# Finishing a batch earlier and splitting a closing check in a log-sum-exp kernel

## The chip, the cores and the metric

The kernel runs on one core of a Trainium2 chip. The metric is device time in microseconds (us). The kernel before took 325.64 us (median of three runs, 325.55 to 325.72).

## What is computed

```python
x_heads = x.reshape(B, S, H, Dh).transpose(0, 2, 1, 3) + bias[None, :, None, :]
x_tiled = np.repeat(x_heads, 2, axis=2)
mx = x_tiled.max(axis=-1, keepdims=True)
lse = mx.squeeze(-1) + np.log(np.exp(x_tiled - mx).sum(axis=-1))
```

B = 8 batches, S = 2048 rows, H = 8 heads of Dh = 256 elements, all float32. For every row and head the logarithm of the sum of exponentials is wanted, and every result is stored twice, side by side. The input has 134 MB, the output 1 MB.

## The kernel before

**Tiles.** A tile is 256 rows: 128 partitions with K = 2 rows each, 2048 elements a row. There are T = 64 tiles, eight to a batch, so batch 6 is tiles 48 to 55 and batch 7 is tiles 56 to 63. SyncE issues all loads into a ring of eight tile buffers (`xb`), and reloads a buffer when its last users are done.

**Work on a tile.** No maximum is subtracted. For some heads TensorE adds the bias: a matmul puts the bias into a bank of PSUM (L336 or L353) and a second one adds x through an identity matrix (L394 or L371). ScalarE then takes the exponential of that bank and sums it through its accumulator (L405, L425). For the other heads of early tiles GpSimd adds the bias (L444) and VectorE sums (L469). In late tiles ScalarE takes the exponential of raw x (L450), and VectorE multiplies by exp(bias) and sums in one instruction for each head (L485, with a read of the accumulator after it). The last head or two go to GpSimd, which multiplies and folds (L501, L509), and VectorE sums the remaining 32 columns (L515). The table `STAGES` gives the shares by tile. From tile 57 on each of the two rows of a partition is a piece of its own (57k0, 57k1 and so on). ScalarE reads the PSUM banks of a piece after the exponential of the next piece. The last tile has eight transfers, with heads loaded in groups.

**Sums.** All sums of a batch collect in a tile `R`: `R0` for batches 0 to 3, `R1` for 4 and 5, `R2` for 6, `R3` for 7. `R3` is ordered by head, tile of the batch, row (k). A group is finished by TensorE transposes, a ScalarE logarithm that writes each result twice, and a store. The first two groups are finished in the stream (`finish`, L529 and L539) and stored after tile 61 (`store`, L544, on SyncE's queue). Batch 6 is finished after the last tile, in `turn_two` (L643) and `finish_two` (L654), and stored from SyncE at L655. Batch 7 is finished in `finish_last` (L663, L670) and stored from ScalarE's queue at L671.

**Closing check.** Since no maximum is subtracted, the kernel checks the range of all sums at the end, and would compute everything again by the safe formula (`all_again`) if it were too wide. `ends_of(i)` takes the maximum (L559) and the minimum (L562) of tile `R`i, as integers, together with those handed on from the tile before, which stand in one padding column at each side of `R`i. The last pair goes to `ends`. `judge` combines them (L578), brings them to one partition with a matmul (L586) and reduces (L587). Then every engine loads the verdict into a register (L590) and branches (L789), and the program ends (L816).

**Order.** The order on every engine is the order of the program text (`manual_schedule`); only semaphores hold engines against each other. `for_pe` and `for_pool` hold work that is put behind the start of the next piece. PSUM has four banks `ps[0..3]` (two tiles `pair` of two banks each), used in turn through the counter `n_ps`. `on_bank` tells the framework that users of different banks of a pair do not depend on each other. `tp` is another bank, for the transposes and for matmuls that only keep TensorE's clock up (L385).

Of the kernel before, what the change touches and what calls it, by code (L numbers as in the profile page):

```python
# [9 lines left out]
F32 = mybir.dt.float32  # L10
BF16 = mybir.dt.bfloat16
I32 = mybir.dt.int32
ACT = mybir.ActivationFunctionType
ALU = mybir.AluOpType
# [3 lines left out]
K = 2  # L18
# [46 lines left out]
def kernel(  # L65
# [6 lines left out]
    nc = tc.nc  # L72
    P = nc.NUM_PARTITIONS
    B, S, D = x.shape
    H, Dh = bias.shape
    assert D == H * Dh and S % (P * KB) == 0
    NBLK = S // (P * K)
    NB = S // (P * KB)
    TB = KB // K
    T = B * NBLK  # L80
# [8 lines left out]
    sb = ctx.enter_context(tc.tile_pool(name="sb", bufs=1))  # L89
# [17 lines left out]
    ends = sb.tile([P, 2], F32, name="ends")  # L107
# [3 lines left out]
    NR = KB * H * NB  # L111
# [3 lines left out]
        starts.append(min(starts[-1] + P // (H * NB), B - 2))  # L115
    groups = list(zip(starts, starts[1:]))
    widths = [(b1 - b0) * NR for b0, b1 in groups] + [NR, NR]
    Rx = [sb.tile([P, 1 + n + 1], F32, name=f"R{i}") for i, n in enumerate(widths)]
    sums_in = [r[:, 1 : 1 + n] for r, n in zip(Rx, widths)]
    R = [  # L120
        r.rearrange("p (k b h n) -> p k b h n", k=KB, h=H, n=NB)[:, :, i]
        for r, (b0, b1) in zip(sums_in, groups)
# [8 lines left out]
    res_two = sb.tile([H * NBLK, P, K, 2], F32, name="res_two")  # L131
    res_last = sb.tile([P, P, 2], F32, name="res_last")
# [7 lines left out]
    ps = [p[:, c : c + MM] for p in pairs for c in (0, MM)]  # L140
    tp = pp.tile([P, KB, P], F32, name="tp")

    def modes_of(t):
        return [modes for t0, modes in STAGES if t0 <= t][-1]
# [92 lines left out]
    for set_idx, (_name, funcs) in enumerate(get_activation_tables(nc.m.arch).items()):  # L237
        if ACT.Exp in funcs and ACT.Ln in funcs:
            nc.scalar.add_instruction(
                mybir.InstLoadActFuncSet(  # L240
                    name=nc.get_next_instruction_name(),
# [30 lines left out]
    for i, c in enumerate(range(G0, D, MM)):  # L272
# [6 lines left out]

    nc.vector.memset(Rx[0][:, 0:1], 1.0)  # L280
    nc.vector.memset(Rx[0][:, 1 + widths[0] :], 1.0)
    nc.vector.memset(one_bits, float(ONE_BITS))
    nc.vector.tensor_reduce(
        out=b_far,
        in_=brow,
        op=ALU.max,
        axis=mybir.AxisListType.X,
# [3 lines left out]
        out=Rx[0][0:1, 1 + widths[0] :],  # L291
# [11 lines left out]
    def other_factors():  # L303
        nc.scalar.activation(
            out=w_ps[:, W_LATE - W0 :], in_=b_rep[:, W_LATE - G0 : W2 - G0], func=ACT.Exp
        )
        nc.scalar.activation(out=w_sb, in_=b_rep[:, W1 - G0 :], func=ACT.Exp)


    n_ps = [0]  # L310
# [4 lines left out]
    def on_bank(i, ins):  # L315
        for j, u in bank_users[i // 2]:
            if j != i and u.ins.engine != ins.ins.engine:
                tc.declare_no_dep(ins.ins, u.ins, reason="another bank")
        bank_users[i // 2].append((i, ins))
        return ins  # L320
# [220 lines left out]
    def store():  # L541

        for (b0, b1), r in zip(groups, res):
            nc.sync.dma_start(  # L544
                out=out[b0:b1].rearrange("b h (n r) -> (b h n) r", n=NB),
                in_=r.rearrange("q p k r -> q (p k r)"),
            )

    def ends_of(i):


        bits = Rx[i].bitcast(I32)
        last = i == len(Rx) - 1
        if not last:
            low = Rx[i + 1][:, 0:1].bitcast(I32)
            high = Rx[i + 1][:, 1 + widths[i + 1] :].bitcast(I32)
        else:
            low, high = ends[:, 0:1], ends[:, 1:2]
        nc.vector.tensor_reduce(  # L559
            out=high, in_=bits[:, 1:], op=ALU.max, axis=mybir.AxisListType.X  # L560
        )
        nc.vector.tensor_reduce(  # L562
            out=low,
            in_=bits[:, 0 : 1 + widths[i]],
            op=ALU.min,
            axis=mybir.AxisListType.X,
            negate=last,
        )

    def begin_row():  # L570
        row = one_ps[0:1, 0:P]
# [25 lines left out]
    def all_again():  # L597
# [10 lines left out]
        with tc.For_i(0, B, 1) as b, tc.For_i(0, S // P, 1) as n:  # L608
# [29 lines left out]
                out=outs[at].rearrange("b n p h r -> (b n p) h r"), in_=both  # L638
            )

    def turn_two():
        for k in range(K):
            nc.tensor.transpose(  # L643
                out=tp[0 : H * NBLK, 1 + k],
                in_=R[B - 2][:, k].rearrange("p h n -> p (h n)"),
                identity=ident,
            )

    def finish_two():
        two = tp[0 : H * NBLK, 1]  # L650
        tv = bass.AP(
            tensor=two.tensor, offset=two.offset, ap=[two.ap[0], [1, P], [P, K], [0, 2]]
        )
        nc.scalar.activation(out=res_two, in_=tv, func=ACT.Ln)  # L654
        nc.sync.dma_start(  # L655
            out=out[B - 2].rearrange("h (n r) -> (h n) r", n=NBLK),
            in_=res_two.rearrange("q p k r -> q (p k r)"),
        )

    def finish_last():  # L660
        bank = n_ps[0] % len(ps)
        last = ps[bank][:, 0:P]
        turn = nc.tensor.transpose(  # L663
            out=last, in_=R_last.rearrange("p h n k -> p (h n k)"), identity=ident
        )
        on_bank(bank, turn)
        tv = bass.AP(
            tensor=last.tensor, offset=last.offset, ap=[last.ap[0], [1, P], [0, 2]]
        )
        on_bank(bank, nc.scalar.activation(out=res_last, in_=tv, func=ACT.Ln))  # L670
        nc.scalar.dma_start(  # L671
            out=out[B - 1].rearrange("h (n r) -> (h n) r", r=2 * P),
            in_=res_last.rearrange("q p r -> q (p r)"),
        )


    def sums_of(t):

        b, blk = divmod(t, NBLK)
        if b < B - 2:  # L680
            return R[b][:, blk % TB * K :, :, blk // TB]
        if b == B - 2:
            return R[b][:, :, :, blk]
        return R_last[:, :, blk, :].rearrange("p h k -> p k h")
# [20 lines left out]
    for t in range(T):  # L705
        if t == T_FACTORS:
            other_factors()
        xt = xts[t % NBUF]
        sums = sums_of(t)
        for k0, k1, c0, c1 in pieces(t):  # L710
            m = modes_of(t)[k0]
            add = None
            heads = []
            if c0 == 0:
                bias_here = bias_there
            if m["late"]:
                pe_part = late_heads(m, t, bias_here, sums)
            else:
                heads = add_x(m, t, k0, c0, c1, bias_here)

                def pe_part(t=t, heads=heads, sums=sums):
                    for k, h, bank, p, mm in heads:
                        sum_biased(t, k, h, bank, p, mm, sums)

            if c0 == 0:
                if next_units and not m["late"]:
                    bias_there = put_bias(*next_units.pop(0))
                if t > T_PROMPT and m["g0"] == H:
                    keep_warm()
                if m["g0"] < H:  # L730
                    add = g_add(m, t, k0, k1)
                if t < T - 1 or k0 == 0:
                    flush(for_pool)
            h0 = max(c0 // Dh, m["pe"])
            h1 = min(c1 // Dh, m["g0"])
            hf = max(h0, min(h1, H - m["fold"]))
            if h0 < h1 and not m["late"]:
                done = exp_inplace(
                    t, xt[:, k0:k1, h0 * Dh : h1 * Dh], loads[t, k0, c0]
                )  # L740
                if hf < h1:
                    for_pool.append(fold(t, k0, hf, h1, sums, done))
            if c0 == 0:
                flush(for_pe)
            if not m["late"]:
                for k in range(k0, k1):
                    for h in range(h0, hf):
                        weigh(
                            t,
                            xt[:, k, h * Dh : (h + 1) * Dh],  # L750
                            h,
                            sums[:, k, h : h + 1],
                            done,
                        )

            def pool_part(t=t, m=m, k0=k0, k1=k1, sums=sums, add=add):
                if add:
                    later(m, t, k0, k1, sums, add)
                if k1 == K:
                    reload(t)  # L760

            for_pool.append(pool_part)
            if m["g0"] < H:
                pe_part()
                if t == T_PROMPT - 1:
                    first_factors()
                if m["late"]:
                    bias_there = put_bias(*next_units.pop(0))
            elif heads:
                for_pe.append(pe_part)  # L770

        for i, (_, b1) in enumerate(groups):
            if t - 2 == b1 * NBLK - 1:
                finish(i)
                ends_of(i)
        if t == T - 3:
            ends_of(len(groups))
            store()
    row = begin_row()
    flush(for_pe)  # L780
    flush(for_pool)
    turn_two()
    finish_two()
    finish_last()
    ends_of(len(groups) + 1)
    again = judge(row) > SPAN_BITS

    order.__exit__(None, None, None)
# [32 lines left out]
```

## Time and profile before

| | |
|---|---|
| time of the runs, median (range) | 325.64 us (325.55 to 325.72) |
| time of the profiled execution | 325.63 us |
| its span, first to last instruction | 323.6 us |
| DMA, mean over the span | 418 GB/s; loads 98.2% of 16 engines' time |
| busy: VectorE, GpSimd, ScalarE, TensorE | 289.1, 287.1, 263.7, 248.0 us |
| last load of x on its way to SBUF until | 317.62 us |
| closing check's last VectorE instruction ends | 320.98 us |
| stores of batch 6 and batch 7, issue to landing | 2.5 and 2.3 us |

Times in the text are microseconds from the start of the span, in that one profiled execution. PE is TensorE, PEld its weight loads, DVE VectorE, ACT ScalarE, POOL GpSimd, SP SyncE; a q behind the name means the engine's instruction queue. L485 is line 485 of the kernel before. A row of the timeline gives start, duration, engine, line, operation, output and input; the note in brackets is idle time of the engine before it and what ended it. On one engine an instruction may start before the one in front of it has ended, so that the distance from start to start, not the duration, is what an instruction costs the next one.

### The profile page before, as it was taken

The page shows a single profiled execution, that of the slowest core. Times are in us where ns is not written, and L with a number is a line of the kernel's source. Part 1 is how long each engine was busy: PE and PEld are TensorE (multiplying, and loading weights), DVE is VectorE, ACT ScalarE, POOL GpSimd, SP SyncE. Part 2 cuts the span into 40 slices and gives each one's busy share as a digit, 9 for nine tenths or more (in the row PEclk, how much of TensorE's full clock was granted, in tenths as well). Part 3 has the DMA queues.
Part 4 walks back from the last instruction along what each step waited for, and adds up shares of the span by engine and source line. Part 5 has one row for each costly group of instructions (what it writes and reads, how often), then busy time and mean ns, then how long its engine had stood idle before and what let it go on. Part 6 is the DMA issues. An engine that isn't in the chain of part 4 may idle for free.

```text
span 323.6 us, 2260 instructions
## 1 busy us (share of the span) xinstructions
PE 248.0 (77%) x601; PEld 98.6 (30%) x601; DVE 289.1 (89%) x322; ACT 263.7 (81%) x422; POOL 287.1 (89%) x121
## 2 busy tenths in 40 slices
PE   5998885877886667887868876987787686398774
PEld 2333332323332223332323332333233322132231
DVE  2337999699989999979999999799999999999996
ACT  1159976798688878598889878799988999889995
POOL 7939997999999999999999989999999999858864
PEclk9979996899799999598999997899999999679998
DMA  7999999999999999999999999999999999999994
GB/s 309 462 397 454 446 398 452 437 405 454 437 405 454 434 407 450 433 413 447 437 406 454 433 407 454 409 423 431 433 425 424 421 438 420 415 421 420 423 401 149
DMA packets 8880, 135.44 MB, mean 418 GB/s; under 512 B 1057, under 2 KB 1441, under 8 KB 2465
## 3 DMA queue, kind: packets, MB, share of 16 engines
q1 hardware_dynamic: 8624, 135.14, 98.2%
q10 hardware_dynamic: 242, 0.14, 0.2%
q8 instruction: 5, 0.08, 0.1%
q14 instruction: 9, 0.07, 0.1%
HBM read 134.23 MB, written 1.05 MB: 418 GB/s over the span
## 4 chain that ended last, share of the span: by engine, by line
DMA 48%; POOL 17%; DVE 15%; PE 10%; ACT 9%; issue 0%; SPq 0%; DVEq 0%
DMA xb<-in_x_dram 48%; POOL xb L444 17%; DVE R L469 11%; ACT xb L450 7%; PE pair L394 4%; PE one_ps L394 2%; DVE xb L462 2%; DVE xb L485 2%; PE pair L336 1%; PE pair L268 1%; ACT xb L412 1%; PE one_ps L336 1%; ACT xb L405 1%; DMA brow<-in_bias_dram 1%; ACT res L539 0%
## 5 line engine op out<-in xcount | busy, mean ns | idle before, releaser
L444 POOL TENSOR_TENSOR xb<-xb,b_rep 128x2048 f32<-128x2048 f32 x57 | 256.8, 4532 | 21.5 <-DMA xb<-in_x_dram 21.5
L469 DVE TENSOR_REDUCE R<-xb 128x14 f32<-128x3584 f32 (+1 forms) x57 | 216.8, 3804 | 1.9
L450 ACT ACTIVATE xb<-xb 128x2560 f32<-128x2560 f32 (+5 forms) x77 | 157.4, 2055 | 20.7 <-POOL xb L444 20.1
L394 PE MATMUL pair<-xb,ident 128*128 128x512 f32 x216 | 111.3, 641 | 0.0
L394 PE MATMUL one_ps<-xb,ident 128*128 128x512 f32 x108 | 62.8, 665 | 18.7 <-DMA xb<-in_x_dram 18.7
L412 ACT ACTIVATE xb<-pair 128x1024 f32<-128x1024 f32 x54 | 55.5, 1028 | 19.1 <-PE pair L394 19.0
L394 PEld LDWEIGHTS pair<-xb,ident 128*128 128x128 f32 x216 | 44.6, 206 | 58.7 <-issue 58.7
L462 DVE TENSOR_TENSOR xb<-xb,w_ps 128x512 f32<-128x512 f32 x54 | 36.7, 680 | 23.0 <-ACT xb L450 23.0
L336 PE MATMUL one_ps<-b,ones_bf 128*128 128x512 bf16 x52 | 20.3, 390 | 36.7 <-ACT xb L405 36.6
L405 ACT ACTIVATE xb<-one_ps 128x256 f32<-128x256 f32 x108 | 39.9, 378 | 7.8 <-PE one_ps L394 7.8
L336 PEld LDWEIGHTS <-ones_bf 128*128 128x128 bf16 (+1 forms) x174 | 17.6, 102 | 86.3 <-issue 79.5
L336 PE MATMUL pair<-b,ones_bf 128*128 128x512 bf16 x104 | 31.2, 381 | 0.0
L371 PE MATMUL pair<-xb,ident 128*128 128x512 f32 (+1 forms) x36 | 21.6, 686 | 12.2 <-DMA xb<-in_x_dram 12.2
L394 PEld LDWEIGHTS one_ps<-xb,ident 128*128 128x128 f32 x108 | 19.9, 201 | 33.4 <-DMA xb<-in_x_dram 27.1
L485 DVE CUSTOM_DVE_ANT_0 xb<-xb,w_ps 128x256 f32<-128x256 f32 x61 | 22.3, 415 | 0.0
L405 ACT ACTIVATION_READ_ACCUMULATOR xb<-one_ps 128x1 f32 x108 | 22.0, 204 | 0.0
L509 POOL TENSOR_TENSOR xb<-xb 128x128 f32<-128x128 f32 (+3 forms) x39 | 13.9, 356 | 3.1
L501 POOL TENSOR_TENSOR xb<-xb,w_sb 128x256 f32<-128x256 f32 (+1 forms) x13 | 10.0, 772 | 5.4 <-ACT xb L450 5.0
L371 PEld LDWEIGHTS pair<-xb,ident 128*128 128x128 f32 x36 | 6.1, 208 | 23.8 <-DMA xb<-in_x_dram 23.3
L425 ACT ACTIVATE xb<-pair 128x256 f32<-128x256 f32 x33 | 12.5, 397 | 0.0
L385 PE MATMUL tp<-b_rep,ident 128*128 128x384 f32 x28 | 11.3, 486 | 0.0
L485 DVE CUSTOM_DVE_ANT_0 xb<-xb,one_ps 128x256 f32<-128x256 f32 x27 | 10.6, 413 | 0.1
(60 smaller groups left out, 72.0 us busy)
## 6 DMA issues: line engine op xcount, KB each, us to landing
xb<-in_x_dram SPq DMA_DIRECT2D x20, 4096.0 KB, 22.1
xb<-in_x_dram SPq DMA_DIRECT2D x17, 2048.0 KB, 22.4
xb<-in_x_dram SPq DMA_DIRECT2D x12, 1024.0 KB, 22.5
xb<-in_x_dram SPq DMA_DIRECT2D x5, 256.0 KB, 11.4
xb<-in_x_dram SPq DMA_DIRECT2D x2, 384.0 KB, 15.8
out_dram<-res SPq DMA_DIRECT2D x1, 512.0 KB, 6.5
out_dram<-res SPq DMA_DIRECT2D x1, 256.0 KB, 6.7
out_dram<-res_two SPq DMA_DIRECT2D x1, 128.0 KB, 2.5
```

Source lines behind the costliest of these rows:

```text
L336: nc.tensor.matmul(p, lhsT=lhsT, rhs=each_row(b, h * Dh, Dh, K), start=i == 0, stop=False,)
L371: mm = nc.tensor.matmul(p, lhsT=ident, rhs=xts[t % NBUF][:, ka:kb, c : c + w], start=False, stop=True,)
L394: mm = nc.tensor.matmul(p, lhsT=ident, rhs=xts[t % NBUF][:, :, h * Dh : (h + 1) * Dh], start=False, stop=True,)
L405: act = nc.scalar.activation(out=xts[t % NBUF][:, k, 0:Dh], in_=got[0][:, k * Dh : (k + 1) * Dh], func=ACT.Exp, accum_out=sums[:, k, 0:1],)
L412: act = nc.scalar.activation(out=xts[t % NBUF][:, :, Dh : m["pe"] * Dh].rearrange("p k (h j) -> p h k j", j=Dh), in_=got[-1].rearrange("p ...
L425: act = nc.scalar.activation(out=xts[t % NBUF][:, k, h * Dh : (h + 1) * Dh], in_=p, func=ACT.Exp, accum_out=sums[:, k, h : h + 1],)
L444: add = nc.gpsimd.tensor_tensor(out=v, in0=v, in1=each_row(b_rep, c - G0, D - c, k1 - k0), op=ALU.add)
L450: return on_x(t, nc.scalar.activation(out=v, in_=v, func=ACT.Exp), [after])
L462: mul = nc.vector.tensor_tensor(out=f, in0=f, in1=each_row(w_ps, m["pe"] * Dh - W0, n, k1 - k0), op=ALU.mult,)
L469: red = nc.vector.tensor_reduce(out=sums[:, k0:k1, h0:H], in_=v.rearrange("p k (h j) -> p k h j", j=Dh), op=ALU.add, axis=mybir.AxisListTy ...
L485: ttr = nc.vector.tensor_tensor_reduce(out=v, in0=v, in1=w, scale=1.0, scalar=0.0, op0=ALU.mult, op1=ALU.add, accum_out=dst,)
L509: done = nc.gpsimd.tensor_tensor(out=v[:, :, 0:n], in0=v[:, :, 0:n], in1=v[:, :, n : 2 * n], op=ALU.add)
```

## The change

- Batch 6 is transposed at the end of the loop's step for tile 59 and its logarithm taken at the end of the step for tile 60. The transposes write to a bank of the ring of four, not to `tp`, so that every later use of the ring moves on by one bank. The store joins the two others in `store`, after tile 61.
- `R3` gets 16 padding columns on each side in place of one, and is set to 1.0 at the start. Its maximum and minimum are taken in two halves: after tile 61 over the columns of tiles 56 to 59, directly behind the pair that hands over batch 6, and at the end over tiles 60 to 63. Each half reads a view of nine groups of eight columns, of which one group is padding with the value handed on.

```diff
-    Rx = [sb.tile([P, 1 + n + 1], F32, name=f"R{i}") for i, n in enumerate(widths)]
+    pads = [1] * (len(widths) - 1) + [NBLK * K]
+    Rx = [sb.tile([P, pad + n + pad], F32, name=f"R{i}") ...
+    nc.vector.memset(Rx[-1], 1.0)
...
+        nc.sync.dma_start(
+            out=out[B - 2].rearrange("h (n r) -> (h n) r", n=NBLK),
+            in_=res_two.rearrange("q p k r -> q (p k r)"),
+        )
...
+    def ends_of_last(half):
+        bits = Rx[-1].bitcast(I32)
+        n = NBLK * K
+        c = half * n // 2
+        views = [
+            bass.AP(
+                tensor=bits.tensor,
+                offset=bits.offset + c0 + c,
+                ap=[bits.ap[0], [n, H + 1], [1, n // 2]],
+            )
+            for c0 in (0, n)
+        ]
+        if half == 0:
+            c = n // 2
+            to = [bits[:, c0 + c : c0 + c + 1] for c0 in (0, n + NR)]
         else:
+            to = [ends[:, 0:1], ends[:, 1:2]]
+        min_max(*views, *to, mybir.AxisListType.XY, last=half == 1)
...
     def turn_two():
+        bank = n_ps[0] % len(ps)
+        n_ps[0] += 1
+        two_in.append(bank)
         for k in range(K):
-            nc.tensor.transpose(
-                out=tp[0 : H * NBLK, 1 + k],
+            turn = nc.tensor.transpose(
+                out=ps[bank][0 : H * NBLK, k * P : (k + 1) * P],
                 in_=R[B - 2][:, k].rearrange("p h n -> p (h n)"),
                 identity=ident,
             )
+            on_bank(bank, turn)
...
+        if t == T - 5:
+            turn_two()
+        if t == T - 4:
+            finish_two()
         if t == T - 3:
             ends_of(len(groups))
+            ends_of_last(0)
             store()
     row = begin_row()
     flush(for_pe)
     flush(for_pool)
-    turn_two()
-    finish_two()
     finish_last()
-    ends_of(len(groups) + 1)
+    ends_of_last(1)
```

`min_max` is a maximum and a minimum by VectorE, one instruction each, as in `ends_of` before. `finish_last` loses its two `on_bank` notes.

More of the change, by code (lines that the diff above doesn't have):

```diff
@@ L117 @@
     widths = [(b1 - b0) * NR for b0, b1 in groups] + [NR, NR]
-    Rx = [sb.tile([P, 1 + n + 1], F32, name=f"R{i}") for i, n in enumerate(widths)]
-    sums_in = [r[:, 1 : 1 + n] for r, n in zip(Rx, widths)]
+    pads = [1] * (len(widths) - 1) + [NBLK * K]
+    Rx = [
+        sb.tile([P, pad + n + pad], F32, name=f"R{i}")
+        for i, (n, pad) in enumerate(zip(widths, pads))
+    ]
+    sums_in = [r[:, pad : pad + n] for r, n, pad in zip(Rx, widths, pads)]
     R = [
@@ L547, in store, with min_max @@
             )
+        nc.sync.dma_start(
+            out=out[B - 2].rearrange("h (n r) -> (h n) r", n=NBLK),
+            in_=res_two.rearrange("q p k r -> q (p k r)"),
+        )
+    def min_max(low_in, high_in, low, high, axis, last=False):
+        nc.vector.tensor_reduce(out=high, in_=high_in, op=ALU.max, axis=axis)
+        nc.vector.tensor_reduce(out=low, in_=low_in, op=ALU.min, axis=axis, negate=last)
     def ends_of(i):
         bits = Rx[i].bitcast(I32)
[L553 to L556, printed above, removed]
-        else:
[L558 to L568, printed above, removed]
+        at = pads[i + 1] + widths[i + 1]
+        min_max(
+            bits[:, 0 : 1 + widths[i]],
+            bits[:, 1:],
+            Rx[i + 1][:, 0:1].bitcast(I32),
+            Rx[i + 1][:, at : at + 1].bitcast(I32),
+            mybir.AxisListType.X,
+        )
[8 more added lines that the diff above has]
+                ap=[bits.ap[0], [n, H + 1], [1, n // 2]],
+            )
+            for c0 in (0, n)
+        ]
+        if half == 0:
+            c = n // 2
+            to = [bits[:, c0 + c : c0 + c + 1] for c0 in (0, n + NR)]
+        else:
+            to = [ends[:, 0:1], ends[:, 1:2]]
+        min_max(*views, *to, mybir.AxisListType.XY, last=half == 1)
     def begin_row():
@@ L639, in all_again @@
             )
+    two_in = []
     def turn_two():
+        bank = n_ps[0] % len(ps)
+        n_ps[0] += 1
+        two_in.append(bank)
         for k in range(K):
-            nc.tensor.transpose(
-                out=tp[0 : H * NBLK, 1 + k],
+            turn = nc.tensor.transpose(
+                out=ps[bank][0 : H * NBLK, k * P : (k + 1) * P],
                 in_=R[B - 2][:, k].rearrange("p h n -> p (h n)"),
@@ L647, in turn_two @@
             )
+            on_bank(bank, turn)
     def finish_two():
-        two = tp[0 : H * NBLK, 1]
+        (bank,) = two_in
+        two = ps[bank][0 : H * NBLK]
         tv = bass.AP(
@@ L653, in finish_two @@
         )
[L654 to L658, printed above, removed]
+        on_bank(bank, nc.scalar.activation(out=res_two, in_=tv, func=ACT.Ln))
     def finish_last():
@@ L662, in finish_last @@
         last = ps[bank][:, 0:P]
-        turn = nc.tensor.transpose(
+        nc.tensor.transpose(
             out=last, in_=R_last.rearrange("p h n k -> p (h n k)"), identity=ident
         )
-        on_bank(bank, turn)
         tv = bass.AP(
@@ L669, in finish_last @@
         )
-        on_bank(bank, nc.scalar.activation(out=res_last, in_=tv, func=ACT.Ln))
+        nc.scalar.activation(out=res_last, in_=tv, func=ACT.Ln)
         nc.scalar.dma_start(
```

## The prediction

> **What bounds the kernel now.** I read the page's time slices first. The DMA row is full up to the last slice, so for 317 us the stream of loads sets the pace; the change does not touch the loads. It touches the last 20 us, so I read the chain that ended last there, then the timelines of ScalarE and VectorE around the places where work goes in, and last what follows the closing check.
>
> ```profile
> DMA  7999999999999999999999999999999999999994
> ```
>
> The chain of waits, in order of time (start, duration, what):
>
> ```profile
> 292.50 19.89 DMA xb<-in_x_dram
> 312.38 0.02 issue
> 312.41 1.71 ACT xb L450
> 314.11 0.02 issue
> 314.14 0.42 DVE xb L485
> ...
> 319.71 0.29 DVE ends L559
> 320.00 0.20 DVE ends L562
> 320.21 0.02 issue
> 320.23 0.17 DVE far L578
> 320.40 0.04 issue
> 320.45 0.23 PE one_ps L586
> 320.68 0.02 issue
> 320.70 0.28 DVE verdict L587
> ```
>
> Piece 62k1 lands at 312.38, its exponential ends at 314.11, and from 314.14 VectorE works without a break through 62k1 and tile 63 until the check. So the end is: landing, one exponential, 5.5 us of VectorE, check. A delay of VectorE at 314.14 goes to the end in full; a delay before 314.14 only beyond the slack there.
>
> The timeline of VectorE shows that slack:
>
> ```profile
> 311.54 0.28 DVE L562 TENSOR_REDUCE R<-R 128x1 int32<-128x129 int32 x1
> 311.74 0.17 DVE L515 TENSOR_REDUCE R<-xb 128x1 f32<-128x32 f32 x1
> 311.83 0.41 DVE L485 CUSTOM_DVE_ANT_0 xb<-xb,one_ps 128x256 f32<-128x256 f32 x1
> ...
> 313.87 0.18 DVE L515 TENSOR_REDUCE R<-xb 128x1 f32<-128x32 f32 x1
> 314.14 0.42 DVE L485 CUSTOM_DVE_ANT_0 xb<-xb,one_ps 128x256 f32<-128x256 f32 x1
> ```
>
> L515 costs the next instruction 0.09 (311.74 to 311.83). After the L515 at 313.87 VectorE could go on at 313.96; it goes on at 314.14, held by ScalarE. **Slack 0.18 us.**
>
> Behind the check (ending 320.98) come the register loads (DVE's, the longest, 957 ns from 321.02), the branches, and SyncE's closing waits (L816). In the trace these stand 0.06 apart from 322.59 to 322.65, but the eighth, on ScalarE's store of batch 7, stands at 322.77, after 0.13: that store lands at 322.76. So the store holds the end by 0.07, and the check is next behind it.
>
> **The change, part by part**, against the profiled 325.63 (span 323.63 and 2.0 around it; the median 325.64 differs by 0.01).
>
> *1. Two reductions added after tile 61, on VectorE, ahead of 311.74.* L559 takes 280, 410 and 677 ns for 129, 257 and 513 columns: 1.03 ns a column. The 129-column pair stands 0.20 apart; 72 columns (nine groups of eight) are 57 fewer, so 0.06 less: 0.14 each, 0.28 together. Each waits for one instruction of the pair in front (maximum for maximum, minimum for minimum). The old maximum ends at 311.62, before the new one could start (311.74); the old minimum ends at 311.82, the new one starts at about 311.88. I take no cost for the waits. Queued behind are L515 of 61k1 and all of tile 62 on VectorE. 0.28 less 0.18 of slack is +0.10; at 316.21 L515 waits 0.02 for GpSimd, which the delay swallows: **+0.08**. Upper bound: each of the new two starts only after its predecessor's end, by the row L562 to L578 (end 320.20, start 320.23). Then the new pair begins at 311.85 and 312.11, L515 follows at 312.25 in place of 311.74, +0.51, and +0.31 is left. Lower bound 0, when the slack covers it; VectorE cannot gain there.
>
> The Trainium skill, "VectorE: DVE Perf Modes", section on the DRAIN, says that the next operation does not start until the pipe is empty. The rows differ: L562 starts at 311.54, 0.08 before L559 ends at 311.62. By that rule this term would be the upper bound.
>
> *2. The last pair reads 72 columns in place of 129.* Start to start 0.06 less for the maximum, 0.06 less until the minimum's end: **-0.12** on the check, nothing on batch 7's store, which does not read `ends`. Bounds -0.12 and 0 (a strided view that costs as much as 129; no strided integer reduce is in the trace, but L485's neighbours L515 and L469, which read several groups, fit the same 1.03 ns, so I take the first).
>
> *3. Batch 6 leaves the end.* Its logarithm (0.60 from 319.32) was not in the way: ScalarE then sat idle 0.17 until TensorE had transposed batch 7. Its store was: its 64 packets of 2 KB run from 321.07 to 322.06, and batch 7's 128 packets of 1 KB from 321.67 to 322.41, some 94 ns long where the median is 46. Alone, eight packets an engine of 46 ns are 0.37, from 321.67 to 322.04, and 0.35 from last packet to landing as now: 322.4, an estimate from these packets. Then the store no longer holds the end and SyncE's eighth wait follows after 0.06: **-0.07**. Bounds: 0 and -0.07, as the check is next.
>
> *4. Batch 6's logarithm goes in on ScalarE ahead of L450 of 61k0.*
>
> ```profile
> 304.91 1.57 ACT L450 ACTIVATE xb<-xb 128x1536 f32<-128x1536 f32 x1
> ...
> 306.91 0.30 ACT L425 ACTIVATION_READ_ACCUMULATOR xb<-pair 128x1 f32 x1
> 307.37 1.48 ACT L450 ACTIVATE xb<-xb 128x1536 f32<-128x1536 f32 x1 [0.16 <-DMA xb<-in_x_dram]
> ...
> 309.86 1.70 ACT L450 ACTIVATE xb<-xb 128x1792 f32<-128x1792 f32 x1 [0.27 <-DMA xb<-in_x_dram]
> ```
>
> A piece costs ScalarE 2.09 and lands every 2.48. An accumulator read costs the next 0.09, so ScalarE is free at 307.00 and waits until 307.37. The logarithm costs about 0.5 (512 columns of L450 at 316.91: 0.52 to the next). 61k0 ends at 306.98, which VectorE wants at 307.84; 61k1 starts at 307.5, 0.12 late, and ends at 308.97, wanted at 309.64; GpSimd's folds shift by as much and are wanted 0.5 later. The next landing, 309.83, absorbs the rest. **0**; without that cover at most the 0.5.
>
> *5. The transposes go in on TensorE before 60k0's matmul.* TensorE idles 0.49 there, from 299.43 to 299.93; the two take 0.41 from first start to last end (318.43 to 318.84). They wait for sums of tile 55 (on VectorE by 293.5) and for 58k1's bank (ScalarE, 298.80). Behind them stand 60k0's matmul and the bias of 60k1, whose bank, moved by one, now waits for 59k0's read at 300.90; it started at 300.89. Nobody wants these results before the next piece, 2 us later. **0**; bounds 0 and 0.1.
>
> *6. Queues.* SyncE issues batch 6's store third in `store`, at about 314.1 (the semaphore it reuses belongs to a load landing at 314.02), 0.47 of issue. No load stands behind it (the last was issued at 309.85); it lands soon after the second store, 319.76. The memset of 160 columns falls at 8.5 us, when VectorE waits for its first tile (21.8). **0**.
>
> Sum: +0.08 - 0.12 - 0.07 = -0.11, so **325.5 us**. With all upper bounds: +0.31 + 0.1 and no gains, 326.0; with all lower ones: -0.19, 325.4.
>
> **Rivals.** A difference under 0.2% (0.65 us) is about what a measurement of this kernel cannot tell from none.
>
> *The new pair on VectorE is dearer than what leaves the end (slower).* Place: the two reductions after tile 61. It decides once they cost over 0.18 + 0.02 + 0.19 = 0.39 where I have 0.28. At the upper bound, 0.51: +0.31 - 0.12 - 0.07 = +0.12, **325.75**; without relief for batch 7's store, +0.31, 325.95. For it: each carries a wait. Against it: what they wait for ends before they can start. Chance 0.22.
>
> *Nothing is gained at the end.* If batch 7's store is as slow alone, it holds the end, and only +0.08 is left: **325.7**. For it: its first packet comes 1.17 after issue, much as batch 6's (1.12), so the contention is only in the later packets. Chance 0.13.
>
> *The loads themselves change.* `R3` grows from 130 to 160 columns, and in the built program every buffer behind it moves 96 bytes: `xb0` starts at byte 60416 of the partition in place of 60320, a multiple of 512 where it was 160 past a multiple of 256. 32 KB packets take 1215 ns and 16 KB ones 613, so 602 for 16 KB and 11 ns for each packet whatever its size. If the place of the buffer makes up 4 ns of that, 8 KB packets go from 313 to 309 (the shortest seen) and 32 KB ones to 1211: 0.3% of some 250 us and 1.3% of the 40 us before the tail: -1.3, **324.3**. Against it: the 48 packets of 96 bytes read from `bparts`, at eight different places modulo 256, all took 12 ns. Chance 0.08; the same shift for the worse 0.04, 326.9.
>
> The Trainium skill, "DMA: Bandwidth & Descriptors", section on AXI transactions, says that a descriptor that does not start at a multiple of 256 bytes costs extra beats. The 48 equal packets do not show it, for reads; no run here shows it for writes.
>
> **How the numbers follow.** The forecast, 325.5, has 0.53, between 325.35 and 325.7; with the two tail rivals 0.88 lies between 325.35 and 326.0. With run-to-run scatter (0.17 among three runs) on both sides I give 325.2 to 326.1. Faster by over 0.2% (below 324.98): 0.08, the shift. Slower (above 326.28): 0.05, the shift the other way and 0.01 for a tail dearer than all bounds. The same: 0.87.
>
> **What would show it.** In the profile after: two integer reductions from 128x72 behind L562's successor, 0.14 apart; L485 of 62k1 about 0.1 after the exponential of 62k1 has ended, not right behind it; the last pair 0.14 apart; batch 7's store landing under 2.1 us after issue; ScalarE's idle time before 61k1 gone and before 62k0 still there. Wrong: a load packet of another length than 1215 or 313 ns, or a VectorE gap before tile 62's last piece.

## The result, and the profile after

The changed kernel takes 323.72 us (median of six) against 325.67 (325.55 to 326.06) measured with it. The ratio is 0.9942, interval 0.9925 to 0.996: faster by 0.6%, outside the range that was given. One execution took 1288.8 us; it counts in the median of six and not in the ratio (the other five are 323.37 to 324.82, their median 323.59), and whether the branch to `all_again` was taken in it no trace shows.

The profiled execution took 323.55 us, with a span of 321.49. I read it from the point where the prediction started, the loads. The page's DMA line of the kernel after:

```profile
DMA  7999999999999999999999999999999999999994
GB/s 303 441 432 457 408 441 451 408 444 432 424 448 413 432 451 416 436 448 417 436 445 424 436 426 424 428 426 430 436 434 427 424 435 432 419 428 425 427 411 174
DMA packets 8880, 135.44 MB, mean 421 GB/s; under 512 B 1057, under 2 KB 1441, under 8 KB 2465
```

The digits are those of before, packets and bytes too, but the mean was 418 GB/s and is 421. A row of tenths cannot show 0.6%: the engines are as busy, the packets are a little shorter. One stretch of the busy times by window shows it as well (last two columns: DMA share, GB/s); first before, then after:

```profile
250.00:300.00 50.00, 36.26 (x86) 13.34 (x84) 49.79 (x94) 46.01 (x73) 43.69 (x27) 0.90 1.01 423
```

```profile
250.00:300.00 50.00, 36.47 (x89) 13.89 (x89) 49.80 (x105) 46.65 (x78) 44.53 (x30) 0.90 1.01 427
```

In the trace's single packets, the mean of a 32 KB packet goes from 1217.6 to 1214.1 ns, of 16 KB from 618.9 to 616.8, of 8 KB from 314.2 to 309.3. Of the 2560 packets of 32 KB, 2551 take exactly 1213 ns after the change; before it 653 do, and most others take 1214 to 1226. The numbers of packets (2560, 2048 and 1792 on 16 engines) make this 0.55, 0.27 and 0.55 us an engine. The last load lands at 315.77 in place of 317.62, piece 62k1 at 310.64 in place of 312.38.

The chain of waits after, in parts (start, duration, what):

```profile
187.34 20.64 DMA xb<-in_x_dram
208.04 4.56 POOL xb L449
212.63 2.35 ACT xb L455
215.00 0.70 DVE xb L467
215.72 3.89 DVE R L474
```

```profile
317.75 0.14 DVE R L520
317.90 0.03 issue
317.93 0.02 DVEq L561
317.95 0.05 issue
318.00 0.23 DVE ends L561
318.22 0.14 DVE ends L562
318.37 0.02 issue
318.39 0.17 DVE far L606
318.56 0.04 issue
318.61 0.23 PE one_ps L614
318.84 0.02 issue
318.86 0.28 DVE verdict L615
```

Before, the chain went back to a load at 292.50. After, its last load is that at 187.34, and from 215.00 to the check it stays on VectorE. Now that the loads are shorter, VectorE is the bound of the last third in this execution.

The new pair of reductions, in VectorE's timeline after (L561 and L562 are the old L559 and L562; L490 was L485, L520 was L515):

```profile
309.55 0.29 DVE L561 TENSOR_REDUCE R<-R 128x1 int32<-128x129 int32 x1
309.75 0.28 DVE L562 TENSOR_REDUCE R<-R 128x1 int32<-128x129 int32 x1
309.94 0.23 DVE L561 TENSOR_REDUCE R<-R 128x1 int32<-128x72 int32 x1
310.08 0.23 DVE L562 TENSOR_REDUCE R<-R 128x1 int32<-128x72 int32 x1
310.21 0.18 DVE L520 TENSOR_REDUCE R<-xb 128x1 f32<-128x32 f32 x1
310.31 0.42 DVE L490 CUSTOM_DVE_ANT_0 xb<-xb,one_ps 128x256 f32<-128x256 f32 x1
```

From 309.94 to 310.21 it costs 0.27. Each of the two lasts 0.23 and holds the next for 0.14 only.

Behind the check, the instructions on the verdict (min/median/max in ns), first before, then after:

```profile
L590 SPq TENSOR_LOAD <-verdict x1: 726/726/726, 321.0 to 321.0; - x1
L590 ACTq TENSOR_LOAD <-verdict x1: 731/731/731, 321.0 to 321.0; - x1
L590 DVEq TENSOR_LOAD <-verdict x1: 957/957/957, 321.0 to 321.0; - x1
```

```profile
L618 SPq TENSOR_LOAD <-verdict x1: 487/487/487, 319.2 to 319.2; - x1
L618 DVEq TENSOR_LOAD <-verdict x1: 581/581/581, 319.2 to 319.2; - x1
L618 ACTq TENSOR_LOAD <-verdict x1: 498/498/498, 319.2 to 319.2; - x1
```

The same register loads take 0.23 to 0.38 less. The span's 2.14 less is then: 62k1 lands 1.74 earlier, VectorE starts on it 0.05 later against that landing, works 0.03 less, the last pair takes 0.12 less, and from the verdict's end to the span's end it is 2.35 in place of 2.65 (0.24 in the register loads, 0.06 in SyncE's last wait).

### The profile page after: what moved, and what is told of

It is laid out like the page before. It is cut to its first block, busy times and chain, and to the rows that moved or that the text cites. A ratio compares the mean times of both kernels' runs of the same rounds, so it can differ in the third digit from the quotient of the medians.

```text
span 321.5 us, 2263 instructions
## 1 busy us (share of the span) xinstructions
PE 243.8 (76%) x600; PEld 97.9 (30%) x601; DVE 289.7 (90%) x325; ACT 263.7 (82%) x422; POOL 288.0 (90%) x121
## 4 chain that ended last, share of the span: by engine, by line
DVE 43%; DMA 35%; PE 9%; ACT 8%; POOL 4%; issue 0%; SPq 0%; DVEq 0%
DMA xb<-in_x_dram 34%; DVE R L474 27%; DVE xb L490 9%; ACT xb L455 6%; POOL xb L449 4%; DVE xb L467 4%; PE pair L399 3%; PE one_ps L399 3%; ACT xb L417 2%; PE pair L272 1%; PE pair L341 1%; ACT xb L410 1%; PE one_ps L341 1%; DMA brow<-in_bias_dram 1%; DVE R L520 0%
## 5 line engine op out<-in xcount | busy, mean ns | idle before, releaser
L399 PE MATMUL pair<-xb,ident 128*128 128x512 f32 x216 | 107.8, 623 | 0.0
L399 PE MATMUL one_ps<-xb,ident 128*128 128x512 f32 x108 | 63.6, 674 | 18.0 <-DMA xb<-in_x_dram 17.8
L490 DVE CUSTOM_DVE_ANT_0 xb<-xb,w_ps 128x256 f32<-128x256 f32 x61 | 22.4, 421 | 0.0
L490 DVE CUSTOM_DVE_ANT_0 xb<-xb,one_ps 128x256 f32<-128x256 f32 x27 | 10.6, 417 | 0.0
```

What stands on the lines that cost most here:

```text
L399: mm = nc.tensor.matmul(p, lhsT=ident, rhs=xts[t % NBUF][:, :, h * Dh : (h + 1) * Dh], start=False, stop=True,)
L490: ttr = nc.vector.tensor_tensor_reduce(out=v, in0=v, in1=w, scale=1.0, scalar=0.0, op0=ALU.mult, op1=ALU.add, accum_out=dst,)
```

## The experiments

Two theories of the 0.6%. **Place**: `R3` is wider, so the load buffers stand 96 bytes further on, at 0 past a multiple of 256 bytes in place of 160, and the packets written there are shorter. **Schedule**: the earlier batch 6 and the split check relieve something that slows the loads or their users.

### The place alone, and the schedule alone

An unused tile ahead of `xbs` moves the buffers; nothing else differs. In the kernel before, 24 columns put them where the change puts them; in the kernel after, 104 columns put them back to 160 past a multiple of 256.

```diff
+    sb.tile([P, 24], F32, name="gap")
     xbs = [sb.tile([P, KB, D], F32, name=f"xb{i}") for i in range(NBUF // TB)]
```

> The kernel before with nothing but an unused tile of 96 bytes ahead of the load buffers, which then start at byte 60416 (a multiple of 512) in place of 60320; everything else stays where it was. If the place of the load buffers shortens the load packets, the last load lands about 1.8 us earlier (315.8 in place of 317.6), the 32 KB packets take 1213 ns throughout, the closing part keeps its 6.0 us, and the time is about 323.8. If the moved work of the change did it, the time stays at 325.6 and the packets stay spread from 1213 to 1221 ns.

> The kernel after with an unused tile of 416 bytes ahead of the load buffers, which then start at byte 60832: 416 past a multiple of 512, as in the kernel before. If the place of the load buffers shortens the packets, the loads are as before (last landing 317.6, packets 1213 to 1221 ns) and only the closing part is shorter, by 0.4 us: about 325.2. If the moved work did it, the time stays at 323.6.

The kernel before with moved buffers took 323.74 us (ratio 0.9943, 0.9929 to 0.9956); the kernel after with buffers put back 325.16 (0.9982, 0.9973 to 0.9991), beside 325.68. The windows, first of the moved kernel before, then of the changed kernel put back:

```profile
250.00:300.00 50.00, 36.40 (x88) 13.60 (x87) 49.79 (x103) 46.52 (x78) 44.42 (x30) 0.90 1.01 427
```

```profile
250.00:300.00 50.00, 35.69 (x87) 13.37 (x86) 49.79 (x101) 46.01 (x74) 43.67 (x28) 0.90 1.01 423
```

427 GB/s goes with the place and not with the schedule. So do the packets: 1214.1 ns for 32 KB moved, 1217.6 put back. The place alone is 1.9 us, as much as the whole change; the schedule alone is 0.5. Together that would be 2.4, and the change gave 1.95; the runs of the two halves below bear on this.

### Which places

The same edit with 8, 16, 56 and 88 columns.

> The kernel before with 32 unused bytes ahead of the load buffers: byte 60352, a multiple of 64 but 192 past a multiple of 256. If a start at a multiple of 64 bytes is enough, the time is that of the run with 96 bytes, about 323.8. If it takes a multiple of 256 (the rule on AXI transactions), it stays at 325.6. If the moved work of the change did it, 325.6 as well.

> The kernel before with 64 unused bytes ahead of the load buffers: byte 60384, 32 past a multiple of 64 as in the kernel before. If the place modulo 64 decides, nothing changes: 325.6. If any move of the buffers against the other tiles helps, it is faster, down to 323.8.

> The kernel before with 224 unused bytes ahead of the load buffers: byte 60544, 128 past a multiple of 512. If a start at a multiple of 128 is enough, the packets are uniform (1213, 611, 309 ns) and the time is about 323.7; if it takes a multiple of 256, 325.7, with packets spread up to 1221 ns.

> The kernel before with 352 unused bytes ahead of the load buffers: byte 60672, a multiple of 256 but not of 512. If a multiple of 256 is enough (the rule on AXI transactions), about 323.7 with uniform packets; if it takes 512, 325.7.

| buffers start, bytes past a multiple of 256 | of 512 | median, us | ratio (interval) | mean of a 32 KB packet, ns |
|---|---|---|---|---|
| 160 (before) | 416 | 325.7 | 1 | 1217.6 |
| 192 | 448 | 325.77 | 1.0004 (0.9995 to 1.0013) | 1217.7 |
| 224 | 480 | 326.02 | 1.0014 (1.0005 to 1.0023) | 1218.7 |
| 128 | 128 | 325.83 | 1.0003 (0.9994 to 1.0012) | 1217.6 |
| 0 | 256 | 323.80 | 0.9942 (0.9927 to 0.9956) | 1214.1 |
| 0 (24 columns) | 0 | 323.74 | 0.9943 (0.9929 to 0.9956) | 1214.1 |

A multiple of 256 bytes is enough, of 128 or 64 is not. The Trainium skill, "DMA: Bandwidth & Descriptors", section "How a descriptor splits into AXI transactions", gives 256 bytes as the boundary from which a descriptor's pieces start, and says that a descriptor that starts elsewhere costs extra beats. The step at 256 agrees with it. But the page speaks of what is read, and here it is the place that is written; and by extra beats alone every packet would be longer, where the last experiment below has packets of 1213.0 ns at 160 past. So the boundary is shown here, and the mechanism behind it is not.

### The two halves of the schedule, with good buffers

The first run takes batch 6 early and leaves the closing check whole; the second splits the check and leaves batch 6 at the end.

```diff
+        if t == T - 5:
+            turn_two()
+        if t == T - 4:
+            finish_two()
...
-    turn_two()
-    finish_two()
```

> The kernel before with the load buffers moved by 96 bytes (323.74 alone) and of the change only its first half: batch 6 transposed, finished and stored early; the closing check is whole. If the store of batch 6, in flight while the engines load the verdict into registers, is what made those loads 0.24 us slower until SyncE's closing waits, and what made the store of batch 7 land 0.06 late, both go: about 323.4, with DVE's register load at 0.58 in place of 0.95 us. If the split check shortened the closing part, 323.7.

> The kernel after (load buffers at the same bytes) with batch 6 finished and stored at the end as before; of the change only the split check is left. The check ends 0.12 - 0.05 = 0.07 earlier, but the store of batch 7 starts 0.05 later and holds SyncE's closing waits: about 323.8, with DVE's register load still near 0.95 us. If the split is what gains, 323.4.

Early batch 6: 323.92 us (323.57 to 325.16; ratio 0.9954, 0.994 to 0.9968). Split check: 324.23 (323.64 to 325.28; 0.9955, 0.994 to 0.9969). Neither is below the place alone, and both expectations were too low. Two things had been missed. The first is the scatter, 1.6 us here: see the kernel after measured again, below. The second is in the verdict's register loads. I had put their 0.24 down to batch 6's store, which is no longer under way beside them. But with batch 6 early and the check whole they are still slow:

```profile
L595 SPq TENSOR_LOAD <-verdict x1: 677/677/677, 319.2 to 319.2; - x1
L595 DVEq TENSOR_LOAD <-verdict x1: 791/791/791, 319.2 to 319.2; - x1
```

There batch 6's store had landed 1.09 before the verdict. With the split check they are short (481 and 535 ns); but that profile is of an execution in which VectorE was late (below), so that batch 6's last packet ended 0.71 before the verdict's end too. What goes with them is when the first packet of batch 7's store runs: 0.41 after the verdict's end with early batch 6, 0.62 with the split check, 0.54 in the kernel after. A register load that starts 0.03 after the verdict and needs 0.48 is done before 0.54, and not before 0.41. That is a new theory: packets of a store beside the register loads make them longer.

### Later store, later verdict

The first run is the kernel with early batch 6 and whole check; ScalarE takes a small logarithm once more ahead of batch 7's store. The second is the kernel after; its last pair reads 144 columns.

```diff
         nc.scalar.activation(out=res_last, in_=tv, func=ACT.Ln)
+        tv = bass.AP(
+            tensor=last.tensor, offset=last.offset, ap=[last.ap[0], [1, 12], [0, 2]]
+        )
+        nc.scalar.activation(out=res_last[:, 0:12], in_=tv, func=ACT.Ln)
```

```diff
-        c = half * n // 2
+        c = 0
...
-                ap=[bits.ap[0], [n, H + 1], [1, n // 2]],
+                ap=[bits.ap[0], [n, H + 1], [1, n // 2 + half * n // 2]],
```

> The kernel before with the buffers moved and batch 6 early, whole check, as in the run of the early batch 6 alone; new is only that ScalarE takes the logarithm of the last batch's first 12 columns twice, so that the store of batch 7 is issued about 0.14 us later. Theory (the register loads of the verdict are slow when the store's packets run beside them): the packets start about 0.55 after the verdict in place of 0.41, SyncE's register load falls from 677 to about 490 ns, DVE's from 791 to about 580, and the span ends 2.35 after the verdict in place of 2.54, so 0.19 EARLIER with more work and a later store. Rival (a store of batch 6 still in flight slows the loads, or the loads are slow for a reason of their own): the loads stay near 680 and 790 ns and the end stays 2.54 after the verdict or moves later by up to 0.14.

> The changed kernel, but its last maximum and minimum read all 144 columns in place of 72: the verdict comes about 0.15 us later, the store of batch 7 as before. Theory (packets beside the register loads): the packets start 0.39 after the verdict in place of 0.54, SyncE's register load grows from 487 to 680 to 720 ns, and the end comes 2.53 after the verdict in place of 2.35: tail +0.34 for 0.15 of work. Rival (the loads are short because batch 6 is stored early): loads stay at 490, tail +0.15.

> The changed kernel as it is, measured again beside the two others. Median 323.4 to 323.8, some executions near 324.8 (VectorE late behind a low TensorE clock). From the end of the verdict to the end of the span 2.35 us in the profile, register loads on SyncE about 487 ns, first packet of batch 7's store 0.54 after the verdict.

The register loads with the later store, then with the later verdict:

```profile
L595 SPq TENSOR_LOAD <-verdict x1: 483/483/483, 319.3 to 319.3; - x1
L595 DVEq TENSOR_LOAD <-verdict x1: 539/539/539, 319.3 to 319.3; - x1
```

```profile
L618 SPq TENSOR_LOAD <-verdict x1: 702/702/702, 319.4 to 319.4; - x1
L618 DVEq TENSOR_LOAD <-verdict x1: 719/719/719, 319.4 to 319.4; - x1
```

First packet 0.58 after the verdict: 483 ns, and the span ends 2.34 behind the verdict (2.54 without the added logarithm). First packet 0.39 after it: 702 ns, and 2.56 behind it. Both as the new theory had it; batch 6's store lands ahead of the verdict in both (by 1.0 and 0.6), so the rival, that this store or something in the loads themselves makes them long, falls. The kernel with the later store took 323.48 us (323.44 to 323.65; ratio 0.9932, 0.9918 to 0.9947), the lowest median of all: more work and a later store, and an end that comes earlier behind the verdict. That is 0.2 of the 0.44 between the medians with and without the added logarithm; the rest is no more than scatter can make. The one with the later verdict took 323.94 (0.9951, 0.9936 to 0.9965).

The kernel after, measured again, took 323.97 (323.85 to 325.36; 0.9955, 0.9939 to 0.997): four executions near 323.9 and two above 325.2, of which the profiled one (span 323.2) is one. Its window from 200 to 250 us (the third column from the right is PEclk, the granted clock), and its VectorE at 62k1:

```profile
200.00:250.00 50.00, 40.61 (x102) 16.82 (x101) 47.34 (x23) 42.91 (x67) 49.38 (x12) 0.93 1.00 429
```

```profile
314.01 0.18 DVE L520 TENSOR_REDUCE R<-xb 128x1 f32<-128x32 f32 x1
314.11 0.42 DVE L490 CUSTOM_DVE_ANT_0 xb<-xb,one_ps 128x256 f32<-128x256 f32 x1
```

In the first profile of the same kernel, that stretch is:

```profile
200.00:250.00 50.00, 37.68 (x101) 15.82 (x100) 49.09 (x23) 43.11 (x67) 49.39 (x12) 1.00 1.00 430
```

With a granted clock of 0.93 in place of 1.00 TensorE needs 2.9 us more for the same work, VectorE is fed later (47.34 busy in place of 49.09) and never catches up: its L490 for 62k1 starts 1.93 after the exponential has ended (312.18), and 0.08 after it in the first profile. The loads landed as early as ever (last one 315.53). The split check's profile is another such execution (0.93 in that stretch, VectorE 1.88 behind). That the clock is the cause is read from these profiles and was not tried by itself. The mean clock of an execution does not decide it: the profiled one had 0.926, and so had one of 323.87 us among the four.

### Are the engines needed for it

In the kernel before, 32 KB packets were 1213.7 ns between 8 and 20 us, when VectorE and ScalarE worked little (2.9 and 3.5 of the 12 us), and 1218.7 between 100 and 200. So a kernel of loads only, in four parts, one execution:

```python
at0 = [sb.tile([P, KB, D], F32, name=f"good{i}") for i in range(2)]
sb.tile([P, 40], F32, name="gap")
at160 = [sb.tile([P, KB, D], F32, name=f"off{i}") for i in range(2)]
...
part, i = divmod(n, PER)
buf = (at0, at160)[part % 2][i % 2]
```

> Only loads of x, 32 of 4 MB in 32 KB packets, in four parts of eight: into two buffers at byte 0 past a multiple of 256, into two at 160 past, and both once more while VectorE, ScalarE and GpSimd work on other buffers (sums of 3584 columns, exponentials of 1536, additions of 2048; nothing depends on them). No log-sum-exp is computed and the stores hold raw x. Theory A (the place costs only beside work of other engines in SBUF): 32 KB packets 1213 ns in the first three parts, 1217 to 1221 in the fourth. Theory B (the place costs in itself, and the early packets of the kernel before were short for another reason): 1217 to 1221 in the second and the fourth part. Theory C (it is the stream's own pattern of transfers and not SBUF): 1213 in all four.

The mean ns of a 32 KB packet, in half parts of some 39 us:

| buffers | engines | first half | second half |
|---|---|---|---|
| 0 past 256 | idle | 1212.9 (without the first 16 packets) | 1213.0 |
| 160 past 256 | idle | 1213.0 | 1216.4 |
| 0 past 256 | busy | 1213.1 | 1213.0 |
| 160 past 256 | busy | 1213.7 | 1216.4 |

The engines begin to work at 168 us, 11 us into the third part, and GpSimd ends at 297.

No theory had this. The engines are not needed: theory A falls. The place costs in itself, as theory B has it, but only some 40 us after the stream began to write to such buffers: from 119.2 us in the second part, which begins at 79.8, and from 274.8 in the fourth, which begins at 234.8. Until then, in the second part, the distance from the start of a packet to that of the sixteenth behind it is 1209, 1210, 1215 or 1216 ns without exception: the 16 transfer engines keep a fixed pattern. From then on four packets in five are longer than 1213 ns, by 1 to 13, the starts drift, and lengths of 1213 to 1226 alternate to the end of the part. Back on buffers at 0 this dies out: the third part takes the drifting starts over, 16 of its packets are 1216 or 1218 ns long, none of them starts behind 158.9 us, and all others are 1213.

The kernel before, looked at again, shows the same: of the 32 KB packets that start before 40 us 25 of 368 are longer than 1213 ns, of those from 45 to 80 us 387 of 458. Of the 25, 20 stand in one row, each starting within 4 ns of the end of the one in front, from a packet of 1264 ns at 13.7 us on; the other packets keep to 1213 until 37.9. The fourth part above has such a row as well (30 long packets, from 236.5 on), the second has none, so a row of this kind is not what sets off the others. How soon they follow goes with the place: the first 4 us in which at least half of the packets are long begin at 44 us with buffers at 160 or 128 past a multiple of 256, at 36 with 192 and at 32 with 224. What disturbs the pattern first, and why it does not settle, is open.

## Why the prediction was wrong, step by step

**The step that failed** is in the rivals: "The loads themselves change", with 0.08 for the gain, and in the opening, "the change does not touch the loads". The place was known (byte 60416 in place of 60320), and so was a price (4 ns a packet, -1.3). I set it low by the 48 packets of 96 bytes that all took 12 ns. Those are reads of SBUF, and of 96 bytes; they could not speak for writes of 32 KB. That 8 KB packets took 313 ns where the shortest seen was 309 went into the price of this rival and not into its chance: lengths scattered upwards from a floor are a cost that could go away. What the runs showed: 32 KB packets 3.5 ns and 8 KB packets 4.9 ns shorter, 1.37 us in the three large sizes and 1.85 at the last landing; what makes up the rest of the 1.85 was not worked out. So the rival had the place right, its odds were wrong, and its size was 0.55 short. It also took the 4 ns as a part of every packet; the runs show packets of 1213 ns at a bad place too, until the pattern breaks.

**Term 1**, the pair at tile 61, +0.08: VectorE starts 0.05 later against the landing. But this is agreement by chance. The pair costs 0.27 (0.28 predicted) and the slack of 0.18 was that of one execution: in the kernel before with moved buffers VectorE is 0.13 late at 62k1 with no pair at all, and in the kernel after with buffers put back it still waits there:

```profile
314.04 0.42 DVE L491 CUSTOM_DVE_ANT_0 xb<-xb,one_ps 128x256 f32<-128x256 f32 x1 [0.24 <-ACT xb L456]
```

**Term 2**, the last pair, -0.12: 0.12, the strided view costs by its columns, as taken.

**Term 3**, batch 6 off the end, -0.07: SyncE's last wait follows after 0.06 and not 0.13, and batch 7's store lands 1.74 after issue:

```profile
out_dram<-res_two SPq DMA_DIRECT2D x1, 128.0 KB, 6.5
out_dram<-res_last ACTq DMA_DIRECT2D x1, 128.0 KB, 1.7
```

What is missing in this term is the register loads, -0.24. I had read them ("DVE's, the longest, 957 ns") and taken them as fixed. The runs give the mechanism, packets of a store beside the loads, and in the profile before there are two such stores: batch 6's packets run from 0.09 to 1.08 after the verdict's end, batch 7's from 0.69 on. Early batch 6 takes the first away, and by itself leaves 677 ns on SyncE; the 0.24 comes only when term 2's earlier verdict lets the loads end before batch 7's packets too. What the split check alone would give is open, since in its one profile batch 6's store was out of the way as well.

**Terms 4 to 6** at 0: the logarithm holds ScalarE for 0.47 (0.5 predicted) from 303.43, and 62k1's exponential still starts 0.03 after its landing; the store of batch 6 is issued at 312.27, third in its queue, and lands at 318.77, ahead of the verdict.

The schedule's sum, -0.11, can be held against the kernel after with buffers put back: 325.16 beside 325.68, -0.52. In the profiles the span is 0.53 shorter: 0.31 behind the verdict (2.34 in place of 2.65), 0.12 in the last pair, and 0.10 because 62k1's exponential starts that much earlier. With good buffers the schedule's part does not show in the medians (323.72, or 323.59 without the odd execution, and 323.97 beside 323.74 and 323.80), as VectorE's scatter is larger; only the profile's end shows it.

The other rivals fell: the pair was not dearer (its starts are 0.14 apart), and the end did gain.

## What to carry to other kernels

Where the stream of loads is the bound, look up in the built program where its buffers start; here a multiple of 256 bytes was worth 0.6%, and an unrelated tile that grew by 30 columns brought it about. Before a change of schedule is credited with a gain, undo the shift of addresses that it brings with a tile that nobody uses. And a slack read from one execution is one sample: when the bound gets shorter, the engine next to it (here VectorE) takes the slack and its scatter becomes the kernel's.

## What was not expected of the hardware

- Writes to buffers off a multiple of 256 bytes lengthen 32 KB packets from 1213 ns to between 1214 and 1226, only after some 30 to 40 us of the stream, and (tried at 160 past) with idle engines too. At a multiple of 256 all but some ten of 2560 packets take 1213.
- A register load of four bytes from SBUF takes 0.48 us on SyncE and 0.54 to 0.58 on VectorE when it is done before a store's packets begin or soon after, and 0.68 to 0.91 and 0.72 to 0.96 when they run beside it. A store issued 0.18 later against the verdict (0.30 in place of 0.48 ahead of it) ended the kernel 0.2 earlier, measured from the verdict.
